# Gain rows of ten norms issued a stage sooner, the third weight chunk after a norm held in written order, and the odd mixer's bounds computed in the memory attention

## The chip, the cores and the metric

The kernel runs on one core of a Trainium2 chip. The metric is the device time of one execution in microseconds. One program computes a whole network for one sequence of 256 tokens; all weights come from device memory.

## What is computed

A residual `x` of 256 x 1024 floats passes two layers of a first block, a norm, two layers of a second block and a last norm. Each sublayer begins with an RMS norm whose gain is a row of 1024 floats.

```python
def rmsnorm(x, g):
    y = x * rsqrt(mean(x * x, axis=-1) + EPS)
    return y * g

# first block, twice: three attention branches, FFN, gated per-layer embedding
h = rmsnorm(x, mix_norm)
z = h @ w_in                       # attention branches a, b, c from z
x = x + (g_a * (o_a @ w_a) + g_b * (o_b @ w_b) + g_c * (o_c @ w_c)) @ w_out
h2 = rmsnorm(x, ffn_norm)          # FFN width 2816 = 22 x 128
x = x + (silu(h2 @ w_gate) * (h2 @ w_up)) @ w_down
x = x + sigmoid(rmsnorm(x, ple_norm) @ w_ple_gate) * (p_i @ w_ple_proj)
# then x = rmsnorm(x, final_norm)

# second block, layer 0 with the even mixer, layer 1 with the odd mixer
x = x + mixer(rmsnorm(x, norm_mix))
x = x + cross_attention(rmsnorm(x, norm_xattn), rmsnorm(mem, norm_mem))
x = x + peer_ffn(rmsnorm(x, norm_ffn))   # 16384 experts, 16 of them per head
# the odd mixer scales its gates with lb = softmax(hgrn_lb_logits, axis 0)[0]
```

## The kernel before

**Matmuls.** Everything is float32. A product is made of three TensorE passes: each operand is split into a rounded part `hi` and a remainder `lo`, and `mm3` issues hi x hi (L305), lo x hi (L306) and hi x lo (L307) into one PSUM bank. A line number as L305 is that of the kernel before.

**Weights.** `chunk` fetches 128 x 1024 floats of a weight (512 KB) by SyncE's queue into one of three `raw` buffers, casts it to `hi` on ScalarE (L289) and subtracts on VectorE to get `lo` (L290, on POOL for some), each again in three buffers. 24 matmuls of 256 columns, or 12 of 512, consume a chunk.

**Two forms of projection.** `lin_a` sums one 512-wide output block over all chunks of its contraction (eight for 1024 inputs) before its consumer runs. `lin_b` gets an output block of 128 features (transposed) out of each chunk, and after each block its `consume` copies from PSUM. The FFN is written like lin_b: for each column f a gate chunk (`ffg`) and an up chunk (`ffu`), 48 matmuls into `fps`, then Silu on ScalarE (L909), the product on VectorE (L910) and the split of the result into `hh` and `hl`; the down chunk of column f comes behind the matmuls of column f+1. In layer 0, `mem_norm` computes the RMS norm of the memory for the second block beside the FFN (Square L378, scaling L380).

**Norms.** Squares of the residual are summed on ScalarE (L420) as blocks of it are finished; v = sum + eps on VectorE (L429), r = v to the power -1/2 on POOL (L431), the scaling `xn = h * r * g` in four instructions on VectorE (L434), then 16 TensorE transposes (L389) into `trp`, and casts and subtractions from PSUM into the pair `xT` (`fTh`, `xTh`, `hTh` by the stage). `norm_t` does all that, and lets `fill` put independent matmuls (the memory's key and value projections) in front of the transposes. The gain row, broadcast to 128 partitions (512 KB), is loaded by `gain` when the norm is written: for most norms into a tile of a pool opened for this norm, whose memory was in use by the stage before; for the two mixers' norms into a `raw` buffer.

**What sets the order.** Code is written stage after stage, and a list scheduler then orders each engine's instructions by a model of their times, so that a weight's cast usually lands far ahead of where it was written. `keep_in_program_order(i)` takes one instruction out of that: it stays behind the instruction written just before it on its own engine. The engines issue strictly in the order so fixed. Memory tiles come from pools on a left and a right side; the residual `h` lies on the right.

**The odd mixer's bounds.** At the start of the odd mixer, L1473 to L1481 make `lb` and 1 - `lb` from two columns of 8 numbers per partition: subtract the maximum, two exponentials on ScalarE (L1476, L1477, with a table load), add, reciprocal, multiply.

Of the kernel before, what the change touches and what calls it, by code (L numbers as in the profile page):

```python
# [10 lines left out]
F32 = mybir.dt.float32  # L11
# [4 lines left out]
AF = mybir.ActivationFunctionType  # L16
OP = mybir.AluOpType
# [3 lines left out]
S, D, P = 256, 1024, 128  # L21
# [173 lines left out]
GAINS = {}  # L195


class Net:
    def __init__(self, ctx, tc, a, out):
        self.tc, self.nc, self.a, self.out = tc, tc.nc, a, out  # L200
        nc = self.nc
# [9 lines left out]
        self.memd = dp.tile([2, P, 8 * S], F32, name="memd")  # L211
        self.kvd = dp.tile([2, P, 4, D], F32, name="kvd")
        self.todo = []
        self.ks = None
        self.open_h()
        ctx.callback(lambda: self.hs.close())
# [12 lines left out]
        lo, hi = COLS["sconv0"][0], sum(COLS["mconvb"])  # L229
# [9 lines left out]
        with self.tc.tile_pool(name="mk", bufs=1) as mk:  # L239
            o, w = CONST["CM"][0], 3 * P  # L240
# [23 lines left out]
    def open_h(self):  # L264
        self.hs = ExitStack()
        hp = self.hs.enter_context(self.tc.tile_pool(name="hp", bufs=1, side="right"))
        self.h = hp.tile([P, 2, D], F32, name="h")

    def bank(self, name):

# [15 lines left out]

    def split(self, src, hi, lo, eng=None):

        self.nc.scalar.copy(out=hi, in_=src)  # L289
        (eng or self.nc.vector).tensor_tensor(out=lo, in0=src, in1=hi.bitcast(F32), op=OP.subtract)  # L290

    def chunk(self, ap, n, raw_only=False, eng=None):

        raw = self.wp.tile([P, 1024], F32, tag="raw", name="raw", bufs=3)
        self.nc.sync.dma_start(out=raw[:, :n], in_=ap)
        if raw_only:
            return raw[:, :n]
        hi = self.wp.tile([P, 1024], F32R, tag="hi", name="hi")
        lo = self.wp.tile([P, 1024], F32R, tag="lo", name="lo")
        self.split(raw[:, :n], hi[:, :n], lo[:, :n], eng)  # L300
        return hi[:, :n], lo[:, :n]

    def mm3(self, ps, lh, ll, rh, rl, start, stop):
# [53 lines left out]
    def rstd(self, ss, n, dim):  # L357
# [5 lines left out]
        nc.gpsimd.tensor_tensor(out=r, in0=v, in1=self.mhalf[:, :n], op=OP.pow)  # L363
        return r

    def gain(self, name, pool=None):
        if name == "mix_norm_0":
            return self.first
        g = self.wp.tile([P, D], F32, tag="raw", name="raw", bufs=3) if pool is None else pool.tile([P, D], F32, tag="gain", name="g", bufs=1)
        j = GAINS[name]  # L370
        self.nc.sync.dma_start(out=g, in_=self.a["gains"][j:j + 1, :].to_broadcast([P, D]))
        return g
# [25 lines left out]
    def norm_t(self, pool, gname, name, fill=0):  # L398
        dst = self.pair(pool, name, 8)
        with self.tc.tile_pool(name="nt", bufs=1) as tp:  # L400
            g = self.gain(gname, None if gname in ('norm_mix_2_0', 'norm_mix_2_1') else tp)
            xs = []
            for t in range(2):
                xs.append(tp.tile([P, D], F32, tag="xn", name="xn", bufs=2))
                self.rms_h(t, g, xs[t])
            fill() if callable(fill) else self.fill(fill)
            for k in range(0, 8, 4):
                for t in range(2):
                    self.trans(xs[t][:, k * P:(k + 4) * P], 4, t, [d[:, k:k + 4] for d in dst])
        return dst  # L410

    def add_h(self, b, t, ps, x=None):
# [178 lines left out]
    def first_layer(self, l):  # L591
        nc, a = self.nc, self.a
        with ExitStack() as st:
# [40 lines left out]
            mT = self.pair(pool("mt"), "mT", 8)  # L634
            for t in range(2):
                self.trans(merged[:, t], 8, t, mT)
            self.lin_a(mT, a[f"wout_{l}"], self.add_h)
        if l:
            self.kv_open(0, "v")
# [294 lines left out]
    def ple(self, l, xp, pr, fill):  # L934
        nc, a = self.nc, self.a
        xT = self.norm_t(xp, f"ple_norm_{l}", "pxT", fill)

        def cg(b, t, ps):
            sl = slice(b * 512, b * 512 + 512)
            g = xp.tile([P, 512], F32, tag="tmp", name="pg", bufs=2)  # L940
            nc.scalar.activation(out=g, in_=ps, func=AF.Sigmoid)
            nc.vector.tensor_tensor(out=g, in0=g, in1=pr[:, t, sl], op=OP.mult)
            self.add_h(b, t, g)
        self.lin_a(xT, a[f"pleg_{l}"], cg)


# [60 lines left out]
    def kv_close(self):  # L1007
        self.fill(1 << 20)
        if self.ks is not None:
            self.ks.close()  # L1010
            self.ks = None

    def mem_attn(self, l):
        nc, a = self.nc, self.a
        with ExitStack() as st:
# [54 lines left out]
            for t in range(2):  # L1070
                turn(0, t, Ps[t])
            Ps = [scores(1, t) for t in range(2)]
            outs(0)
            outs(1)
            for t in range(2):
                turn(1, t, Ps[t])
            outs(2)
            outs(3)
            self.lin_a(oT, a[f"xwo_{l}"], self.add_h)

    def softplus(self, pool, x, w):
# [32 lines left out]
    def even_mixer(self, xp, hT):  # L1114
# [48 lines left out]
        def project():  # L1163
            for kt in range(16):
# [4 lines left out]
                                 hi[:, n * 512:n * 512 + 512], lo[:, n * 512:n * 512 + 512], kt == 0, kt == 15)  # L1169
                yield 1  # L1170
        out = project()
        with st:
            self.ssd(sp_, c, hT, dt, cs, lg, yT, xb, xbc)
        with ExitStack() as st:
# [290 lines left out]
    def odd_mixer(self, xp, hT):  # L1465
        nc, a = self.nc, self.a
        with ExitStack() as st:
            pl = st.enter_context(self.tc.tile_pool(name="hg", bufs=1))
            c = self.tables(pl, "m01", "rst")

            T8 = lambda n: pl.tile([P, 8], F32, name="lb_" + n)
            mx, e0, e1, lb, ob = T8("m"), T8("0"), T8("1"), T8("b"), T8("o")
            nc.vector.tensor_tensor(out=mx, in0=self.col["lb0"], in1=self.col["lb1"], op=OP.max)  # L1473
            nc.vector.tensor_tensor(out=e0, in0=self.col["lb0"], in1=mx, op=OP.subtract)
            nc.vector.tensor_tensor(out=e1, in0=self.col["lb1"], in1=mx, op=OP.subtract)
            nc.scalar.activation(out=e0, in_=e0, func=AF.Exp)  # L1476
            nc.scalar.activation(out=e1, in_=e1, func=AF.Exp)  # L1477
            nc.vector.tensor_tensor(out=e1, in0=e0, in1=e1, op=OP.add)
            nc.vector.reciprocal(e1, e1)
            nc.vector.tensor_tensor(out=lb, in0=e0, in1=e1, op=OP.mult)  # L1480
            nc.vector.tensor_scalar(ob, lb, -1.0, 1.0, op0=OP.mult, op1=OP.add)  # L1481
            big = lambda n: pl.tile([P, 8, S], F32, name=n)
            f, k, q = big("hf"), big("hk"), big("hq")

# [128 lines left out]
            self.lin_a(oT, a["od_out"], self.add_h)  # L1613


# [227 lines left out]
```

## Time and profile before

| | us |
|---|---|
| three runs | 3420.84, 3422.93, 3423.55 (median 3422.93) |
| profiled execution, its own time | 3420.93 |
| its span | 3419.2 |
| TensorE busy | 3283.9 (96%) |
| VectorE busy | 2251.0 (66%) |
| ScalarE busy | 1759.0 (51%) |
| DMA, mean over the span | 167 GB/s |

TensorE is the busy engine; 570 MB of weights stream beside it. A busy share is a mean over all stages. PE is TensorE's matmul, DVE VectorE, ACT ScalarE, SP SyncE, which issues the DMAs. "Granted clock" is the share of TensorE's full clock (2.4 GHz; half of it is 1.2 GHz) that it got in a stretch. In rows of instructions, the bracket at a row's end is how long that engine stood idle before it, and what ended the idle time.

### The profile page before, as it was taken

Reading aid. Unit: us, or ns where it says so; the run is one execution under the profiler, and the core shown is the slowest. Engines: PE = TensorE matmul, PEld = TensorE weight load, DVE = VectorE, ACT = ScalarE, POOL = GpSimd, SP = SyncE. Lnnn points to the kernel's source line nnn. Section 1 sums busy time; section 2 is a strip of 40 time slices with the busy share of each in tenths; the row PEclk is TensorE's granted clock in tenths of the full one; section 3 lists DMA queues with packets and bytes.
Section 4 is the critical chain, followed back from the end, with each engine's and each line's share of the span. In section 5 each row is a group of like instructions: output and inputs, shape, how many; then the busy total and the mean of one; then the engine's idle time right before and its main releaser. Section 6 shows DMA issues by size and latency. Waiting matters only on the chain.

```text
span 3419.2 us, 53950 instructions
## 1 busy us (share of the span) xinstructions
PE 3283.9 (96%) x20870; PEld 2901.5 (85%) x20870; DVE 2251.0 (66%) x3881; ACT 1759.0 (51%) x3222; POOL 240.1 (7%) x159
## 2 busy tenths in 40 slices
PE   8999999989999999989999999999999899999999
PEld 6768998767997988888988999988888898899998
DVE  6666556756556776589965555567658996555555
ACT  4545445544445554445954444456444495444444
POOL 0000000000000000065000000000005500000000
PEclk9999999989999999999999999999999999999999
DMA  5345666445555345543255555555544315555555
GB/s 188 114 141 188 221 205 193 133 130 169 174 188 180 132 156 175 174 141 124 72 192 186 188 188 186 189 192 174 183 156 148 124 58 192 189 186 189 186 187 177
DMA packets 161105, 570.00 MB, mean 167 GB/s; under 512 B 18256, under 2 KB 23760, under 8 KB 159824
## 3 DMA queue, kind: packets, MB, share of 16 engines
q1 hardware_dynamic: 160848, 566.56, 50.1%
q8 instruction: 163, 2.67, 0.3%
q14 instruction: 94, 0.77, 0.1%
HBM read 557.05 MB, written 9.44 MB: 166 GB/s over the span
## 4 chain that ended last, share of the span: by engine, by line
PE 62%; DVE 11%; ACT 2%; DMA 1%; issue 1%; POOL 0%; DVEq 0%; POOLq 0%; ACTq 0%; SPq 0%
PE pacc L305 7%; PE pacc L307 7%; PE pacc L306 7%; PE aps L305 5%; PE aps L306 4%; PE aps L307 4%; PE ps L307 3%; PE ps L305 3%; PE ps L306 3%; PE gps L1697 3%; PE ps L1690 2%; PE fps L305 1%; PE fps L306 1%; PE fps L307 1%; DVE G L1783 1%
## 5 line engine op out<-in xcount | busy, mean ns | idle before, releaser
L290 DVE TENSOR_TENSOR lo<-raw,hi 128x1024 fp32r<-128x1024 f32 (+3 forms) x906 | 1102.3, 1218 | 769.7 <-ACT hi L289 764.9
L289 ACT CAST hi<-raw 128x1024 fp32r<-128x1024 f32 (+1 forms) x978 | 1019.1, 1044 | 919.5 <-issue 213.8
L305 PE MATMUL pacc<-hi,pwh 128*128 128x512 f32 x1024 | 404.4, 395 | 0.1
L307 PE MATMUL pacc<-hi,pwl 128*128 128x512 f32 x1024 | 403.7, 394 | 0.0
L306 PE MATMUL pacc<-lo,pwh 128*128 128x512 f32 x1024 | 402.9, 393 | 0.0
L305 PE MATMUL aps<-xTh,hi 128*128 128x256 f32 x1296 | 365.2, 282 | 0.9 <-ACT G L1700 0.9
L306 PE MATMUL aps<-xTl,hi 128*128 128x256 f32 x1296 | 365.0, 282 | 0.0
L307 PE MATMUL aps<-xTh,lo 128*128 128x256 f32 x1296 | 363.7, 281 | 0.0
L305 PE MATMUL ps<-xTh,hi 128*128 128x256 f32 x960 | 277.0, 289 | 16.4 <-ACT hi L289 12.5
L307 PE MATMUL ps<-xTh,lo 128*128 128x256 f32 x960 | 276.4, 288 | 15.2 <-POOL lo L290 15.2
L289 ACT CAST pwh<-G 128x256 fp32r<-128x256 f32 x256 | 103.9, 406 | 342.6 <-DVE G L1705 213.8
L306 PE MATMUL ps<-xTl,hi 128*128 128x256 f32 x960 | 275.5, 287 | 1.2 <-DVE xTl L290 1.2
L305 PEld LDWEIGHTS aps<-xTh,hi 128*128 128x128 f32 x1296 | 243.8, 188 | 7.8 <-ACT G L1700 1.3
L306 PEld LDWEIGHTS aps<-xTl,hi 128*128 128x128 f32 x1296 | 243.7, 188 | 7.2
L307 PEld LDWEIGHTS aps<-xTh,lo 128*128 128x128 f32 x1296 | 243.8, 188 | 0.0
L307 PEld LDWEIGHTS pacc<-hi,pwl 128*128 128x128 f32 x1024 | 192.4, 188 | 45.7 <-DVE pwl L290 0.3
L305 PEld LDWEIGHTS pacc<-hi,pwh 128*128 128x128 f32 x1024 | 192.6, 188 | 39.1 <-ACT pwh L289 1.0
L306 PEld LDWEIGHTS pacc<-lo,pwh 128*128 128x128 f32 x1024 | 193.1, 189 | 37.9
L290 POOL TENSOR_TENSOR lo<-raw,hi 128x1024 fp32r<-128x1024 f32 x72 | 192.4, 2681 | 179.1 <-ACT hi L289 178.6
L305 PE MATMUL fps<-fTh,hi 128*128 128x256 f32 x704 | 199.6, 284 | 4.8 <-ACT fTh L289 4.8
L305 PEld LDWEIGHTS ps<-xTh,hi 128*128 128x128 f32 x960 | 186.2, 194 | 18.1 <-ACT hi L289 13.3
L307 PEld LDWEIGHTS ps<-xTh,lo 128*128 128x128 f32 x960 | 186.3, 194 | 16.5 <-POOL lo L290 16.3
(653 smaller groups left out, 6958.0 us busy)
## 6 DMA issues: line engine op xcount, KB each, us to landing
raw<-in_pu_dram SPq DMA_DIRECT2D x256, 512.0 KB, 3.3
raw<-in_pv_dram SPq DMA_DIRECT2D x256, 512.0 KB, 3.3
raw<-in_wbg_dram SPq DMA_DIRECT2D x48, 512.0 KB, 3.6
raw<-in_ffg_dram SPq DMA_DIRECT2D x44, 512.0 KB, 3.6
raw<-in_ffu_dram SPq DMA_DIRECT2D x44, 512.0 KB, 3.4
raw<-in_ffd_dram SPq DMA_DIRECT2D x44, 512.0 KB, 3.8
raw<-in_win_dram SPq DMA_DIRECT2D x36, 512.0 KB, 3.3
raw<-in_pwq_dram SPq DMA_DIRECT2D x32, 512.0 KB, 3.3
```

The costliest lines, as they stand in the source:

```text
L289: self.nc.scalar.copy(out=hi, in_=src)
L290: (eng or self.nc.vector).tensor_tensor(out=lo, in0=src, in1=hi.bitcast(F32), op=OP.subtract)
L305: mm(ps, lhsT=lh, rhs=rh, start=start, stop=False)
L306: mm(ps, lhsT=lh, rhs=rl, start=False, stop=False)
L307: mm(ps, lhsT=ll, rhs=rh, start=False, stop=stop)
L1690: nc.tensor.matmul(pi, lhsT=w[:, k * P:k * P + P], rhs=xT32[:, k], start=k == 0, stop=k == 7)
L1697: nc.tensor.matmul(ps[:, t * P:t * P + P], lhsT=A[:, t], rhs=B[:, t], start=True, stop=True)
L1783: nc.vector.tensor_tensor(out=cv[:, h], in0=vv[:, h, 0, :, None].to_broadcast([P, 16, 16]), in1=vv[:, h, 1, None, :].to_broadcast([P, 16, ...
```

## The change

1. `gain_ahead(name)` loads a norm's gain row into one buffer that lies in the pool of the residual, and `gain` later takes it from there. It is called for ten of the fifteen rows that `gain` loads: the ffn and ple norms of both layers, the second layer's first norm (`mix_norm_1`), `final_norm`, and the query and PEER norms of the second block. The call stands before the last projection of the stage ahead of the norm (for the ple norm, behind the FFN's norm; for the query norm of layer 0, ahead of the even mixer's recurrences).
2. `norm_t` sets a counter to zero at its end; `chunk` counts, and keeps cast and subtraction of the third chunk in written order on their engines.
3. The odd mixer's bounds move into `lower_bounds`, called in the memory attention of the second block's first layer, between the scores of its second head and the outputs of its first; the two exponentials are held in written order there. 

```diff
@@ chunk
-        self.split(raw[:, :n], hi[:, :n], lo[:, :n], eng)
+        ins = self.split(raw[:, :n], hi[:, :n], lo[:, :n], eng)
+        self.since += 1
+        if self.since == 3:
+            for i in ins:
+                self.tc.keep_in_program_order(i)
@@
+    def gain_ahead(self, name):
+        g = self.hp.tile([P, D], F32, tag="gain", name="g", bufs=1)
+        j = GAINS[name]
+        self.nc.sync.dma_start(out=g, in_=self.a["gains"][j:j + 1, :].to_broadcast([P, D]))
+        self.ahead[name] = g
@@ gain
+        if name in self.ahead:
+            return self.ahead.pop(name)
@@ norm_t, at its end
+        self.since = 0
@@ calls, each ahead of the projection beside it
+            self.gain_ahead(f"ffn_norm_{l}")
             self.lin_a(mT, a[f"wout_{l}"], self.add_h)
...
             xT = self.norm_t(xp, f"ffn_norm_{l}", "fT", fill)
+            self.gain_ahead(f"ple_norm_{l}")
...
+        self.gain_ahead("final_norm" if l else "mix_norm_1")
         self.lin_a(xT, a[f"pleg_{l}"], cg)
...
+            self.gain_ahead(f"norm_ffn_2_{l}")
             self.lin_a(oT, a[f"xwo_{l}"], self.add_h)
...
         out = project()
+        self.gain_ahead("norm_xattn_2_0")
...
+            self.gain_ahead("norm_xattn_2_1")
             self.lin_a(oT, a["od_out"], self.add_h)
@@ mem_attn
             Ps = [scores(1, t) for t in range(2)]
+            if l == 0:
+                self.lower_bounds()
             outs(0)
@@ odd mixer
-            mx, e0, e1, lb, ob = T8("m"), T8("0"), T8("1"), T8("b"), T8("o")
-            nc.vector.tensor_tensor(out=mx, in0=self.col["lb0"], in1=self.col["lb1"], op=OP.max)
...
-            nc.scalar.activation(out=e0, in_=e0, func=AF.Exp)
-            nc.scalar.activation(out=e1, in_=e1, func=AF.Exp)
...
+            lb, ob = self.lbs
```

The number of instructions stays the same on all engines but ScalarE, which has one table load less. The order changes around the norms. In the rows below `hi<-raw` is a weight's cast, `lo<-raw,hi` its subtraction; the code's later lines stand a few further down in the changed kernel (L289 is L292 there, L909 is L930, L290 is L293, L1030 is L1068).

ScalarE at the FFN of layer 0, from the casts of the normed input on, before:

```order
L289 CAST fTh<-trp 128x4x128 x4
L289 CAST hi<-raw 128x1024 x2
L378 ACTIVATE xn,ss<-mem 128x1024
L289 CAST hi<-raw 128x1024
L909 ACT_TABLE_LOAD
L909 ACTIVATE sg<-fps 128x256
L378 ACTIVATE xn,ss<-mem 128x1024
L289 CAST hh<-sg 128x256
L289 CAST hi<-raw 128x1024 x2
```

and in the changed kernel:

```order
L292 CAST fTh<-trp 128x4x128 x4
L396 ACTIVATE xn,ss<-mem 128x1024
L930 ACT_TABLE_LOAD
L930 ACTIVATE sg<-fps 128x256
L396 ACTIVATE xn,ss<-mem 128x1024
L292 CAST hh<-sg 128x256
L292 CAST hi<-raw 128x1024 x5
```

The casts of column 1's gate and up chunk (and of column 0's down chunk) stood ahead of Silu of column 0; now they stand behind `hh` of column 0.

ScalarE at the query projection of the second block's layer 0 (`xTh` is the normed input, `mqT` the copy of one 128-feature block of queries), before:

```order
L289 CAST xTh<-trp 128x4x128 x4
L289 CAST hi<-raw 128x1024
L1030 ACTIVATE mqT<-ps 128x256
L289 CAST hi<-raw 128x1024 x2
L1030 ACTIVATE mqT<-ps 128x256
L289 CAST hi<-raw 128x1024
L1030 ACTIVATE mqT<-ps 128x256
```

and in the changed kernel:

```order
L292 CAST xTh<-trp 128x4x128 x4
L1068 ACTIVATE mqT<-ps 128x256 x2
L292 CAST hi<-raw 128x1024 x3
L1068 ACTIVATE mqT<-ps 128x256
L292 CAST hi<-raw 128x1024 x2
L1068 ACTIVATE mqT<-ps 128x256
```

The third chunk's cast stood ahead of the first block's copy; now it stands behind the second block's.

VectorE in the even mixer, around `lg`, the last step of the softplus chain (`sp_q` are its steps, `cacc` and `xb` those of a convolution), before:

```order
L290 TENSOR_TENSOR lo<-raw,hi 128x1024
L1095 SCALAR_TENSOR_TENSOR sp_q<-sp_q,sp_z_10615 128x40
L1112 SCALAR_TENSOR_TENSOR xb<-xpad,cacc 128x256
L1096 SCALAR_TENSOR_TENSOR sp_q<-sp_q,sp_z 128x40
L1108 TENSOR_SCALAR cacc<-xpad,cl 128x256
L1097 SCALAR_TENSOR_TENSOR sp_q<-sp_q,sp_m 128x40
L1110 SCALAR_TENSOR_TENSOR cacc<-xpad,cl,cacc 128x256
L1151 TENSOR_TENSOR lg<-sp_q,na 128x2x16
L1152 TENSOR_SCALAR lg<-sp_q 128x2x4
```

and in the changed kernel:

```order
L1136 SCALAR_TENSOR_TENSOR sp_q<-sp_q,sp_z_10615 128x40 x3
L1153 SCALAR_TENSOR_TENSOR xb<-xpad,cacc 128x256
L1137 SCALAR_TENSOR_TENSOR sp_q<-sp_q,sp_z 128x40
L1138 SCALAR_TENSOR_TENSOR sp_q<-sp_q,sp_m 128x40
L1192 TENSOR_TENSOR lg<-sp_q,na 128x2x16
L1193 TENSOR_SCALAR lg<-sp_q 128x2x4
L293 TENSOR_TENSOR lo<-raw,hi 128x1024 x3
```

The subtractions of chunks 3 to 5 were spread among the chain's steps; now all three stand behind `lg`.

## Rows read from the trace of the kernel before

**Rows 1.** Page: the span, and the engines' busy time, share and instructions.
```profile
span 3419.2 us, 53950 instructions
PE 3283.9 (96%) x20870; PEld 2901.5 (85%) x20870; DVE 2251.0 (66%) x3881; ACT 1759.0 (51%) x3222; POOL 240.1 (7%) x159
```
**Rows 2.** Page, costliest groups: count, busy us, mean ns; idle time before and releaser.
```profile
L290 DVE TENSOR_TENSOR lo<-raw,hi 128x1024 fp32r<-128x1024 f32 (+3 forms) x906 | 1102.3, 1218 | 769.7 <-ACT hi L289 764.9
L289 ACT CAST hi<-raw 128x1024 fp32r<-128x1024 f32 (+1 forms) x978 | 1019.1, 1044 | 919.5 <-issue 213.8
```
**Rows 3.** Windows: length; busy us of PE, PEld, DVE, ACT, POOL; granted clock; DMA.
```profile
309.50:321.40 11.90, 11.75 (x96) 11.49 (x96) 5.96 (x9) 7.54 (x12) 0.55 (x1) 1.00 0.87 304
848.60:854.90 6.30, 1.90 (x18) 1.68 (x17) 2.23 (x4) 3.60 (x7) 0.00 (x0) 0.83 0.67 222
854.90:860.40 5.50, 5.49 (x27) 5.25 (x28) 1.66 (x3) 0.22 (x1) 0.00 (x0) 0.57 0.29 95
...
1085.00:1094.00 9.00, 4.82 (x32) 4.28 (x31) 7.38 (x15) 6.88 (x17) 1.23 (x4) 0.87 0.50 154
...
1412.00:1430.00 18.00, 15.36 (x123) 14.52 (x122) 14.27 (x18) 8.82 (x16) 1.07 (x2) 1.00 0.84 289
...
2530.00:2541.00 11.00, 3.67 (x17) 3.07 (x17) 6.90 (x12) 3.82 (x9) 1.06 (x2) 0.69 0.76 244
```
**Rows 4.** Timeline of ACT, FFN of layer 0: start and length in us.
```profile
309.84 1.09 ACT L289 CAST hi<-raw 128x1024 fp32r<-128x1024 f32 x1
...
316.31 1.06 ACT L378 ACTIVATE xn<-mem 128x1024 f32<-128x1024 f32 x1 [2.34 <-DMA mem<-in_mem_dram]
...
318.42 1.28 ACT L909 ACT_TABLE_LOAD   x1
319.71 0.39 ACT L909 ACTIVATE sg<-fps 128x256 f32<-128x256 f32 x1
...
321.04 0.39 ACT L289 CAST hh<-sg 128x256 fp32r<-128x256 f32 x1
```
**Rows 5.** Timeline of DVE, same stretch.
```profile
320.13 0.42 DVE L910 TENSOR_TENSOR sg<-sg,fps 128x256 f32<-128x256 f32 x1 [0.47 <-ACT sg L909]
...
321.81 1.28 DVE L380 SCALAR_TENSOR_TENSOR xn<-mem,r,g 128x1024 f32<-128x1024 f32 x1
```
**Rows 6.** Timeline of POOL, same stretch.
```profile
321.47 0.83 POOL L363 TENSOR_TENSOR r<-v,mhalf 128x1 f32<-128x1 f32 x1 [3.12 <-DVE v L361]
```
**Rows 7.** Groups of ACT by form: count, busy us, mean ns.
```profile
L1030 ACT ACTIVATE mqT<-ps 128x256 f32<-128x256 f32 x16 | 6.0, 377 | 0.0
...
L1486 ACT ACTIVATE hf<-ps 128x256 f32<-128x256 f32 x8 | 3.1, 384 | 0.7 <-PE ps L307 0.7
```
**Rows 8.** Timeline of DVE, final norm and even mixer's start.
```profile
1084.56 2.74 DVE L434 SCALAR_TENSOR_TENSOR h<-h,r,g 128x512 f32<-128x512 f32 x4 [3.83 <-DMA g<-in_gains_dram]
...
1108.96 1.22 DVE L290 TENSOR_TENSOR lo<-raw,hi 128x1024 fp32r<-128x1024 f32 x1
...
1115.69 0.18 DVE L1151 TENSOR_TENSOR lg<-sp_q,na 128x32 f32<-128x32 f32 x1
```
**Rows 9.** Timeline of ACT, FFN of layer 1.
```profile
851.87 1.04 ACT L289 CAST hi<-raw 128x1024 fp32r<-128x1024 f32 x1 [2.66 <-DMA raw<-in_ffg_dram]
```
**Rows 10.** Timeline of DVE, PEER norm of layer 1.
```profile
2534.81 2.74 DVE L434 SCALAR_TENSOR_TENSOR xn<-h,r,g 128x512 f32<-128x512 f32 x4 [3.02 <-DMA g<-in_gains_dram]
```
**Rows 11.** Timeline of POOL, same norm.
```profile
2531.81 1.06 POOL L431 TENSOR_TENSOR r<-v,mhalf 128x1 f32<-128x1 f32 x2 [75.05 <-DVE v L429]
```
**Rows 12.** Timeline of PE, query projection of layer 1.
```profile
2466.89 0.62 PE L305 MATMUL ps<-xTh,hi 128*128 128x256 f32 x3 [0.68 <-ACT xTh L289]
2468.37 0.39 PE L306 MATMUL ps<-xTl,hi 128*128 128x256 f32 x1 [0.86 <-DVE xTl L290]
```
**Rows 13.** Timeline of ACT, odd mixer's start.
```profile
2303.17 1.04 ACT L289 CAST hi<-raw 128x1024 fp32r<-128x1024 f32 x1 [1.35 <-DMA raw<-in_od_f_dram]
```
**Rows 14.** Waits of PE: us in total, times, longest.
```profile
PE psb L307 <- DVE lo L290: 4.3, 4, 1.7
```

More of the change, by code (lines that the diff above doesn't have):

```diff
@@ L213, in __init__ @@
         self.todo = []
+        self.since = 0
+        self.ahead = {}
         self.ks = None
@@ L267, in open_h @@
         self.h = hp.tile([P, 2, D], F32, name="h")
+        self.hp = hp
     def bank(self, name):
@@ L287, in split @@
     def split(self, src, hi, lo, eng=None):
-        self.nc.scalar.copy(out=hi, in_=src)
-        (eng or self.nc.vector).tensor_tensor(out=lo, in0=src, in1=hi.bitcast(F32), op=OP.subtract)
+        h = self.nc.scalar.copy(out=hi, in_=src)
+        l = (eng or self.nc.vector).tensor_tensor(out=lo, in0=src, in1=hi.bitcast(F32), op=OP.subtract)
+        return h, l
     def chunk(self, ap, n, raw_only=False, eng=None):
@@ L409, in norm_t @@
                     self.trans(xs[t][:, k * P:(k + 4) * P], 4, t, [d[:, k:k + 4] for d in dst])
+        self.since = 0
         return dst
@@ L1011, in kv_close, with lower_bounds @@
             self.ks = None
+    def lower_bounds(self):
+        nc = self.nc
+        T8 = lambda n: self.cp.tile([P, 8], F32, name="lb_" + n)
+        mx, e0, e1, lb, ob = T8("m"), T8("0"), T8("1"), T8("b"), T8("o")
+        nc.vector.tensor_tensor(out=mx, in0=self.col["lb0"], in1=self.col["lb1"], op=OP.max)
+        nc.vector.tensor_tensor(out=e0, in0=self.col["lb0"], in1=mx, op=OP.subtract)
+        nc.vector.tensor_tensor(out=e1, in0=self.col["lb1"], in1=mx, op=OP.subtract)
+        for e in (e0, e1):
+            self.tc.keep_in_program_order(nc.scalar.activation(out=e, in_=e, func=AF.Exp))
+        nc.vector.tensor_tensor(out=e1, in0=e0, in1=e1, op=OP.add)
+        nc.vector.reciprocal(e1, e1)
+        nc.vector.tensor_tensor(out=lb, in0=e0, in1=e1, op=OP.mult)
+        nc.vector.tensor_scalar(ob, lb, -1.0, 1.0, op0=OP.mult, op1=OP.add)
+        self.lbs = lb, ob
     def mem_attn(self, l):
@@ L1469, in odd_mixer @@
             c = self.tables(pl, "m01", "rst")
-            T8 = lambda n: pl.tile([P, 8], F32, name="lb_" + n)
-            mx, e0, e1, lb, ob = T8("m"), T8("0"), T8("1"), T8("b"), T8("o")
-            nc.vector.tensor_tensor(out=mx, in0=self.col["lb0"], in1=self.col["lb1"], op=OP.max)
-            nc.vector.tensor_tensor(out=e0, in0=self.col["lb0"], in1=mx, op=OP.subtract)
-            nc.vector.tensor_tensor(out=e1, in0=self.col["lb1"], in1=mx, op=OP.subtract)
-            nc.scalar.activation(out=e0, in_=e0, func=AF.Exp)
-            nc.scalar.activation(out=e1, in_=e1, func=AF.Exp)
[L1478 to L1481, printed above, removed]
+            lb, ob = self.lbs
             big = lambda n: pl.tile([P, 8, S], F32, name=n)
```

## Prediction

> **What bounds the kernel now.** I read the page's busy times first. TensorE is busy for 96% of a span of 3419.2 us [rows 1], so the change can move the time only where TensorE stands still or where its clock falls. Next I asked for the cost of feeding it. Each weight chunk needs one cast on ScalarE (1.04 us) and one subtraction on VectorE (1.22 us), 978 and 906 times [rows 2], before its third matmul can run. Matmul work per 128x1024 chunk is 2.86 us: the 96 matmuls of two FFN columns ran in 11.90 us with only a short wait at their start, 0.119 us each [rows 3]. So both feeders are faster than TensorE as long as they may run ahead, and a feeder that must not run ahead costs TensorE a full chain of cast and subtraction. Then I went through the places that the diff touches, norm by norm, and asked there which wait ends last. The profiled execution took 3420.93 us; the median of the runs is 3422.93, 2 us more, inside their spread of 2.7.
>
> **The pin on the third chunk.** The pin puts cast and subtraction of the third chunk after a norm behind whatever was written just before on the same engine. In the projections that sum over eight chunks (ple gate, input projection) that is the second chunk, and nothing waits; I price those at 0. In the others the consumer of the first two chunks is written before the third one, so the third chunk can now only be cast when TensorE has finished all it has. That holds at eight places.
>
> *FFN of layer 0.* In the trace the cast of chunk 3 runs at 309.84, long before Silu at 319.71 [rows 4], and TensorE never stops between f=0 and f=1. Afterwards the ScalarE order is Square of mem, table load, Silu, Square, hh, then this cast. The first Square began at 316.31 when its DMA landed [rows 4], which is after the 48 matmuls of f=0 end (about 315.6, half of the 96 [rows 3]). So: Square to 317.4, table load 1.28 to 318.7, Silu 0.39 to 319.1, a second Square (1.06) to 320.1, hh 0.39 to 320.5, cast 1.05 to 321.4 (starts overlap by 0.1). VectorE has in front of its subtraction the product with Silu (0.42), two scalings of mem (1.28 each), hl, and a power on POOL that the second scaling needs (0.83) [rows 5, 6]: product to 319.5, scaling to 320.8, hl to 321.2, power to 322.2, scaling to 323.4, subtraction to 324.6. The third matmul of f=1 could have run at 315.9: **+8.8**. If mem landed early and only Silu, product, hh, hl, power, scaling and subtraction stood in a row the price would be 5.4; with mem's DMA a load later, 10.3.
>
> By that row the table load holds ScalarE for 1.28 and Silu starts 0.01 later. The Trainium skill (ScalarE: Activation LUTs, What ACT_TABLE_LOAD costs) adds a drain of 1.38 us to every switch. By it this term would be 10.2 and the sum 1.4 larger; the trace shows no such drain here, and I go by the trace.
>
> *FFN of layer 1.* No mem work there: Silu 0.39, product 0.42, hh 0.39, cast 1.05, subtraction 1.22, less two matmuls that need only the cast (0.24), and 0.3 for hand-overs: **+3.5**.
>
> *The two query projections and the two PEER projections.* One copy of a 128x256 PSUM block (0.38 [rows 7]), cast 1.05, subtraction 1.22, less 0.24: 2.4, with the hand-over 2.5, four times: **+10.0**. Bounds 2.2 and 2.9 each.
>
> *Odd mixer.* hf and hk (0.38 each [rows 7], overlapping to 0.66) ahead of cast and subtraction: **+2.8**.
>
> *Even mixer.* ScalarE isn't held, VectorE is: the subtraction of chunk 3 now stands behind lg, the end of the softplus chain. In the trace that subtraction ran at 1108.96 and lg at 1115.69 [rows 8]. This eats what the norm gives there; it is priced with the norm below.
>
> **The gain rows loaded ahead.** The 512 KB rows are the same, ten of fifteen are issued one stage sooner. It matters where the scaling waited for its row, or where the third chunk's cast stood ahead of the transposes' casts.
> - FFN of layer 1: TensorE works 1.90 of the 6.30 us from 848.60 [rows 3], because a weight cast that waited 2.66 for its DMA stands on ScalarE ahead of fTh [rows 9]. The pin takes that cast away: fTh can follow the transposes, **-4.0**. The half clock behind this wait (27 matmuls in 5.50 us where 0.119 each would be 3.2 [rows 3]) goes too: **-2.3**.
> - Even mixer: final_norm's scaling waited 3.83 for its row until 1084.56 [rows 8]. Early by about that, the transposes and the first xbc chunk move forward by 5. But chunk 2 is then late by its DMA, and chunk 3 waits for lg, which I work out to 1107.3 (about 12 softplus steps after chunk 2's first matmuls, interleaved with the convolution): chunk 3's matmuls start at about 1108.5, and by chunk 5 the lead is gone: **0**, bounds -5 and +4.
> - PEER of layer 1: the scaling waited 3.02 for its row until 2534.81, r was there at 2532.9 [rows 10, 11]. Gain at least 1.9, at most 3.9 (without the cast and the subtraction that ran ahead of the squares and of v): **-3.5**, nearer to the upper end since both are pinned away.
> - PEER of layer 0 and queries of layer 1, the same cast out of the way: **-0.9**, and **-1.6** (the waits of 0.68 and 0.86 [rows 12]).
> - The other norms didn't wait for their rows: 0. The issue costs SP 0.3 to 0.4 us each as before; a row that goes out ahead of a weight chunk can delay it, which I keep for the range (+0 to +2).
>
> **The odd mixer's bounds.** Seven tiny VectorE steps, two exponentials and a table load of 1.28 leave the odd mixer's start. ScalarE waited for a weight DMA there until 2303.17 [rows 13], so nothing becomes earlier: 0. In the memory attention they stand beside other exponentials: 0.
>
> **The clock.** New stalls can cost more than their length. TensorE fell to the half clock behind the 4.4 us of idle time before 854.90 (a granted 0.57 in the 5.5 us after it); the 9 us from 1085 with 4.2 idle show 0.87; the 18 us from 1412, with 2.6 idle in several pieces, stay at 1.00 [rows 3]. I take 2.3 behind the long stall of FFN 0, as measured there, 1.7 behind the shorter one of FFN 1, and 1.0 for the four of 2.5 together, which lie between the two cases: **+5**.
>
> **Sum.** Losses 8.8 + 3.5 + 10.0 + 2.8 = 25.1; gains 4.0 + 2.3 + 3.5 + 0.9 + 1.6 = 12.3; clock 5. 3420.9 + 25.1 - 12.3 + 5 = 3438.7. Against a median that lies 2 us above the profiled execution it would be 3440.7; the measured runs reach down to 3420.84, so I give **3438**.
>
> **Rivals.**
> 1. *No change.* The even mixer keeps its lead of 5, no new stall lowers the clock, FFN 0 costs its lower bound: 3438.7 - 5 - 5 - 3.4 = 3425. For it: the stretch with 2.6 idle at 1.00. Against it: the subtraction behind lg.
> 2. *Faster.* The place is the front of four norms. All that TensorE loses there goes: in FFN 1 6.3, in the even mixer about 10 (4.2 of the 9 us from 1085, the four waits of psb on its subtractions, 4.3 together [rows 14], and the clock), in PEER 1 7.3 of the 11 us from 2530 [rows 3], 2.5 in PEER 0, 1.5 in the queries: 28. The pins' stalls are at their lower bounds, 5.4 + 3.2 + 4 x 2.2 + 2.5 = 20. That gives 3413. It decides from gains of about 27 on; against it stands that a norm has squares, v, r, scaling, transposes and casts in a row even with its row at hand, so PEER 1 can't lose its whole 7.3.
> 3. *The clock falls behind each new stall.* Besides the two FFN stalls the other six cost 1.7 each instead of 1.0 together: 3438.7 + 9 = 3448. The rows with 0.87 and with 1.00 lie on both sides of such a stall.
>
> The Trainium skill (TensorE: Matmul & The Clock Gate, What's actually happening) says that the gate goes by how busy the array was of late; by that alone rival 3 would hold wherever a stall is long enough, and the traced stretch at 1.00 shows that short ones are free.
>
> **How the numbers follow.** Chances: the forecast 0.53, rival 3 0.15, no change 0.20, faster 0.12. The range: from the lower bounds (no clock loss, FFN 0 at 5.4, even mixer -5, PEER gain 3.9) 3424, lowered to 3420 to take in the no-change case; from the upper ones (FFN 0 at 10.3, even mixer +4, PEER gain 1.9, clock +9 more) 3455, cut to 3452 since they won't all come together. About what a measurement of this kernel can tell from no change is 0.2%, 6.8 us: faster 0.12, within 0.20, slower 0.68.
>
> **What would show it.** Right: in the changed kernel's trace a TensorE wait of 8 to 9 us on a subtraction in FFN 0 right after f=0, with the weight cast after hh; waits of about 2.5 on lo in both query and both PEER projections; the wait before FFN 1's first matmul gone and one of 3.5 three us later; final_norm's scaling starting at once on its row, and a wait on lo behind lg. Wrong: the third chunk's casts before the consumers, or TensorE waits there under 1 us; then the gains stand alone and the kernel is faster.

## The result, and the profile after

The changed kernel took 3440.43 us in the median of four runs (3438.8 to 3446.18), the kernel before 3421.89 (3420.62 to 3423.55): 1.0057 of before, 95% interval 1.0042 to 1.0071. It is 18.5 us slower; 3438 was forecast. The profiled execution has a span of 3437.0 us against 3419.2 [rows 1].

Page of the changed kernel, the span and the engines' busy time:

```profile
span 3437.0 us, 53932 instructions
PE 3295.3 (96%) x20870; PEld 2909.9 (85%) x20870; DVE 2253.1 (66%) x3881; ACT 1758.0 (51%) x3221; POOL 239.6 (7%) x159
```

The engines do the same work as in [rows 1]; TensorE's busy time is 11.4 us longer with the same 20870 matmuls, at a mean granted clock of 0.980 instead of 0.984: more of them ran at the half clock. Thus 11.4 of the 17.8 us between the two spans are matmuls that took longer, and 6.4 are time in which TensorE stood idle. Where the time went is found by comparing the start of the same matmul in two traces (the n-th of 20870) at the borders of the stages. Each number is how much longer, in us, a stage took than in the trace of the kernel before; the column "idle" is the part of it in which TensorE stood still (the stage's length less PE's busy time in it), and the rest is matmuls that took longer:

| stage (us of before) | changed | of it idle | forecast | before, profiled again |
|---|---|---|---|---|
| FFN of layer 0 (308 to 330) | +9.4 | +7.0 | +8.8, clock +2.3 | -0.3 |
| FFN of layer 1 (845 to 880) | 0.0 | -1.3 | -6.3 +3.5, clock +1.7 | -0.7 |
| final norm and even mixer's start (1074 to 1125) | +3.8 | +0.6 | 0 | -0.2 |
| queries of layer 0 (1345 to 1385) | +0.8 | +0.7 | +2.5 | +0.1 |
| PEER norm and projection 0 (1412 to 1450) | +2.5 | +0.9 | -0.9 +2.5 | +0.2 |
| odd mixer's start (2301 to 2345) | +5.7 | +2.1 | +2.8 | +1.5 |
| queries of layer 1 (2440 to 2500) | -0.6 | -0.8 | -1.6 +2.5 | -0.1 |
| PEER norm and projection 1 (2525 to 2565) | -0.4 | -1.3 | -3.5 +2.5 | +0.5 |

These add to +21.2, of which 8.0 are idle time and 13.2 longer matmuls. The other stages gave back 3.4, which makes up the 17.8 between the two spans; in the second trace of the unchanged kernel they gave back 3.3 too, so that lies in the trace of before and not in the change. The last column says how to take such numbers: it is the unchanged kernel against itself (experiment e10). Stages without an edit differ there by 1.2 (start), -2.4 (compressed keys of layer 1) and -2.5 (routing of layer 1), and the odd mixer by 1.5.

**FFN of layer 0.** Timeline of ScalarE in the changed kernel (start, length, idle time before it and what ended it), to be held against [rows 4]:

```profile
317.20 1.06 ACT L396 ACTIVATE xn<-mem 128x1024 f32<-128x1024 f32 x1 [6.39 <-DMA mem<-in_mem_dram]
...
318.36 1.28 ACT L930 ACT_TABLE_LOAD   x1
319.66 0.38 ACT L930 ACTIVATE sg<-fps 128x256 f32<-128x256 f32 x1
...
320.98 0.39 ACT L292 CAST hh<-sg 128x256 fp32r<-128x256 f32 x1
321.27 1.99 ACT L292 CAST hi<-raw 128x1024 fp32r<-128x1024 f32 x2
```

VectorE there, and TensorE:

```profile
322.82 1.28 DVE L398 SCALAR_TENSOR_TENSOR xn<-mem,r,g 128x1024 f32<-128x1024 f32 x1 [0.73 <-POOL r L372]
324.02 2.35 DVE L293 TENSOR_TENSOR lo<-raw,hi 128x1024 fp32r<-128x1024 f32 x2
```

```profile
316.42 0.28 PE L316 MATMUL fps<-fTh,lo 128*128 128x256 f32 x1
322.37 0.58 PE L314 MATMUL fps<-fTh,hi 128*128 128x256 f32 x1 [5.67 <-ACT hi L292]
...
324.26 0.79 PE L314 MATMUL facc<-hi,hh 128*128 128x512 f32 x1 [1.10 <-ACT hi L292]
325.29 0.58 PE L316 MATMUL fps<-fTh,lo 128*128 128x256 f32 x1 [0.24 <-DVE lo L293]
```

The raw chunk lay ready, but ScalarE stood 6.39 us for mem's DMA, and only behind Square, table load, Silu, the second Square and hh came the cast at 321.27, which had been at 309.84 [rows 4]. The subtraction waited for mem's second scaling. The third matmul of column 1 came at 325.29; without a wait it would have been due three matmuls after 316.42, at 316.78: 8.5 us, where 8.8 were worked out.

**FFN of layer 1.** ScalarE in the changed kernel:

```profile
857.17 2.06 ACT L292 CAST fTh<-trp 128x512 fp32r<-128x512 f32 x4
859.24 1.28 ACT L930 ACT_TABLE_LOAD   x1
865.01 0.38 ACT L930 ACTIVATE sg<-fps 128x256 f32<-128x256 f32 x1 [4.49 <-PE fps L316]
...
866.19 2.94 ACT L292 CAST hi<-raw 128x1024 fp32r<-128x1024 f32 x3
```

TensorE there:

```profile
867.28 0.58 PE L314 MATMUL fps<-fTh,hi 128*128 128x256 f32 x1 [2.31 <-ACT hi L292]
...
868.54 0.58 PE L316 MATMUL fps<-fTh,lo 128*128 128x256 f32 x1 [0.47 <-DVE lo L293]
```

The wait in front of fTh [rows 9] is gone, and the casts of column 1 come behind Silu and hh instead. Both are worth 6 us, so nothing is left of the gain.

**Clock.** Windows of the changed kernel (length; busy us of PE, PEld, DVE, ACT, POOL; granted clock; DMA):

```profile
316.55:325.20 8.65, 1.74 (x5) 0.79 (x3) 4.55 (x8) 6.98 (x10) 1.10 (x2) 0.76 0.15 62
325.20:332.00 6.80, 6.71 (x46) 6.71 (x47) 3.54 (x4) 1.05 (x1) 0.00 (x0) 0.80 0.69 231
...
864.40:872.00 7.60, 4.82 (x23) 4.33 (x23) 4.34 (x5) 3.63 (x5) 0.00 (x0) 0.69 0.31 87
...
2327.00:2332.50 5.50, 5.50 (x34) 5.49 (x34) 3.01 (x5) 1.81 (x4) 0.00 (x0) 0.69 0.71 234
```

Behind each of the three longer stalls (both FFNs, odd mixer) TensorE ran part of the following work at the half clock: 46 matmuls took 6.71 us in the second window where 0.119 each would be 5.5, and 34 took 5.50 in the last one where they would be 4.0.

### The profile page after: what moved, and what is told of

Its sections match the earlier page's. It is cut to its first block, busy times and chain, and to the rows that moved or that the text cites. A ratio compares the mean times of both kernels' runs of the same rounds, so it can differ in the third digit from the quotient of the medians.

```text
span 3437.0 us, 53932 instructions
## 1 busy us (share of the span) xinstructions
PE 3295.3 (96%) x20870; PEld 2909.9 (85%) x20870; DVE 2253.1 (66%) x3881; ACT 1758.0 (51%) x3221; POOL 239.6 (7%) x159
## 4 chain that ended last, share of the span: by engine, by line
PE 61%; DVE 11%; ACT 2%; DMA 1%; issue 1%; POOL 0%; DVEq 0%; POOLq 0%; ACTq 0%; SPq 0%
PE pacc L314 7%; PE pacc L316 7%; PE pacc L315 7%; PE aps L314 5%; PE aps L315 4%; PE aps L316 4%; PE ps L314 3%; PE ps L316 3%; PE ps L315 3%; PE gps L1729 3%; PE ps L1722 2%; PE fps L316 1%; PE fps L315 1%; PE fps L314 1%; DVE G L1815 1%; ACT hi L292 1%
## 5 line engine op out<-in xcount | busy, mean ns | idle before, releaser
L293 DVE TENSOR_TENSOR lo<-raw,hi 128x1024 fp32r<-128x1024 f32 (+3 forms) x906 | 1101.5, 1218 | 769.0 <-ACT hi L292 763.8
L292 ACT CAST hi<-raw 128x1024 fp32r<-128x1024 f32 (+1 forms) x978 | 1018.2, 1044 | 883.9 <-issue 210.5
L292 ACT CAST pwh<-G 128x256 fp32r<-128x256 f32 x256 | 103.8, 406 | 342.2 <-DVE G L1737 213.9
L293 POOL TENSOR_TENSOR lo<-raw,hi 128x1024 fp32r<-128x1024 f32 x72 | 191.6, 2672 | 181.6 <-ACT hi L292 131.6
L316 PE MATMUL fps<-fTh,lo 128*128 128x256 f32 x704 | 200.0, 284 | 0.7 <-DVE lo L293 0.7
```

The source lines that it names most:

```text
L292: h = self.nc.scalar.copy(out=hi, in_=src)
L293: l = (eng or self.nc.vector).tensor_tensor(out=lo, in0=src, in1=hi.bitcast(F32), op=OP.subtract)
L316: mm(ps, lhsT=ll, rhs=rh, start=False, stop=stop)
```

## Experiments

All ratios are against the kernel before on the same chip, with 95% intervals. Stage numbers are differences to the trace of before, as in the table above.

**e1: the gain rows alone.** The changed kernel without its pin, and with the odd mixer's bounds where they were.

```diff
-        self.since += 1
-        if self.since == 3:
-            for i in ins:
-                self.tc.keep_in_program_order(i)
```

> The kernel before with the gain rows of the ten norms loaded ahead, no pin, bounds where they were. Theory A (the pins make the loss, the rows give a gain): the waits for gain rows in front of final_norm and of both PEER norms go, and the order ahead of the second FFN and of the second queries is cleared as well: 6 to 12 us faster than before, 3410 to 3416. Theory B (the rows issued ahead get in the way of weight loads, the pins cost nothing): 10 us or more slower than before.

Measured: 0.9988 (0.9979 to 0.9997). Theory A has the sign, but the gain is 3.4 us of 3422.85 and not 6 to 12. By stages: FFN 1 -6.3 as worked out, the even mixer's start +4.9 where a gain was expected, PEER 0 +1.6, PEER 1 -0.3. ScalarE at FFN 1 in this run:

```profile
849.30 2.05 ACT L292 CAST fTh<-trp 128x512 fp32r<-128x512 f32 x4
853.05 1.05 ACT L292 CAST hi<-raw 128x1024 fp32r<-128x1024 f32 x1 [1.69 <-DMA raw<-in_ffg_dram]
```

So the cast of [rows 9] that stood ahead of fTh moves behind it without any pin. With the gain row loaded ahead the scheduler orders the two the other way by itself.

The even mixer is the surprise. Its scaling and lg (VectorE), its first chunks and `cps`, the first matmul that needs lg (TensorE), and windows of the whole stage and of two stretches in it:

```profile
1073.81 2.74 DVE L449 SCALAR_TENSOR_TENSOR h<-h,r,g 128x512 f32<-128x512 f32 x4 [0.61 <-POOL r L446]
...
1112.94 0.18 DVE L1170 TENSOR_TENSOR lg<-sp_q,na 128x32 f32<-128x32 f32 x1
```

```profile
1092.98 0.39 PE L310 MATMUL psb<-hTh,hi 128*128 128x256 f32 x1 [1.67 <-ACT hi L292]
1095.46 0.58 PE L310 MATMUL psb<-hTh,hi 128*128 128x256 f32 x1 [1.75 <-ACT hi L292]
1113.25 1.04 PE L1175 MATMUL cps<-lg,cst 128*128 128x20 f32 x4 [3.86 <-DVE lg L1171]
```

```profile
1068.11:1123.99 55.88, 46.25 (x335) 43.94 (x334) 42.38 (x91) 28.76 (x56) 2.81 (x11) 0.88 0.52 164
1094.40:1101.10 6.70, 5.64 (x26) 5.64 (x27) 3.49 (x9) 2.59 (x5) 0.10 (x1) 0.50 0.74 229
1113.20:1118.00 4.80, 4.75 (x22) 4.75 (x23) 2.79 (x10) 0.42 (x1) 0.00 (x0) 0.50 0.30 106
```

The same stage in the kernel before:

```profile
1074.02:1125.01 50.99, 42.97 (x335) 40.51 (x333) 40.97 (x90) 28.97 (x56) 3.72 (x11) 0.97 0.53 171
```

The scaling no longer waits for its row (0.61 for r instead of 3.83 for the DMA [rows 8]). Yet TensorE is idle for 9.6 us of the stage instead of 8.0, and busy with the same 335 matmuls for 46.2 instead of 43.0. Behind the two waits for casts it gets through the chunks that are written ahead of cps without the later waits of [rows 14], and then stands 3.86 us in one piece for lg. VectorE makes lg even later, 44.8 us after the stage's start, where it was 41.7 before [rows 8]. The half clock follows in two places, behind the two waits of 1.67 and 1.75 (0.50 from 1094.40 to 1101.10) and behind the long one (0.50 from 1113.20 on).

**e2: the pin alone.** The kernel before with the counter and the pin, rows and bounds as before.

> The kernel before with the pin of the third chunk alone. Theory A: stalls of TensorE at the first FFN (about 9), the second FFN, the odd mixer (3 to 6) and both PEER projections (2.5 each), less what the casts give that no longer stand ahead of the norm's own casts: 15 to 25 us slower than before, 3437 to 3447. Theory B: within 3 us of before.

Measured: 1.0068 (1.0054 to 1.0081), 23.1 us: theory A. Stages: FFN 0 +9.7, FFN 1 -0.1, even mixer's start +4.3, PEER 0 +2.1, odd mixer +5.0, PEER 1 +2.5, queries +0.9 and -0.6. At FFN 1 the pin alone also takes away the wait of [rows 9]; the casts of column 1 come behind hh:

```profile
859.78 2.05 ACT L292 CAST fTh<-trp 128x512 fp32r<-128x512 f32 x4
...
868.79 2.94 ACT L292 CAST hi<-raw 128x1024 fp32r<-128x1024 f32 x3
```

The even mixer loses 4.3 us to the pin alone, 4.9 to the row alone and 3.8 to both, so the losses don't add. In all three TensorE waits for lg (2.33 here, 3.86 in e1, 2.27 in the changed kernel), and the stage's granted clock is 0.88 to 0.91 instead of 0.97.

**e3: the odd mixer's bounds alone.**

> The kernel before with the odd mixer's bounds made in the memory attention, nothing else. Theory A: ScalarE waits for a weight load at the odd mixer's start anyway, so within 2 us of before. Rival: the table load that goes was on the path to the second weight cast there, 1.3 to 2.5 us faster.

Measured: 1.0003 (0.9993 to 1.0012), the odd mixer's start -0.1. The table load taken off ScalarE buys nothing, since the next weight comes by DMA at its own time [rows 13].

**e4: the pair held behind the norm's own casts.** The pinned pair follows the last cast and subtraction of the norm's transposes, not what was written just before it.

```diff
-            for i in ins:
-                self.tc.keep_in_program_order(i)
+            for i, p in zip(ins, self.norm_last):
+                if i.ins.engine == p.ins.engine:
+                    self.tc.add_manual_dep(i.ins, p.ins.name, ...)   # issue order only
```

> The changed kernel with one thing different: cast and subtraction of the third chunk are held behind the last cast and subtraction of the norm's own transposes, and no longer behind the consumers of the first two chunks. Theory A: all stalls of the pins go and all gains stay: 8 to 15 us faster than before, 3407 to 3414. Theory B: as slow as the changed kernel, 3437 to 3443.

Measured: 0.9981 (0.9972 to 0.9990), 6.2 us faster than before, less than the 8 to 15 expected. In its trace the even mixer keeps its loss (+4.2) and a new one turns up in the attention of layer 1 (+4.9, e9). They are the likely reason, but not a shown one: the traced execution, 3410.01, is the fastest of eleven and lies where it was expected with both losses in it. All pins' stalls are gone: FFN 0 -0.1, FFN 1 -6.0, odd mixer -0.1, queries -0.1 and -1.4.

**e5: the changed kernel without the pin in the two FFNs.**

> The changed kernel with the pin left out in the two FFNs only. If the FFN pins cost what the stages of the traces say (9.4 in layer 0, 6.2 in layer 1 against the run with gain rows alone), this is 15 to 16 us faster than the changed kernel: 3424 to 3426. By the prediction's own terms (8.8 + 2.3 and 3.5 + 1.7) it would be 16.3. If instead the time lost is made up elsewhere (the later FFN columns), less than 8.

Measured: 1.0012 (1.0003 to 1.0021), that is 0.0045 of 3424 or 15 us below the changed kernel, as the stages say (FFN 0 -0.1, FFN 1 -5.9). The FFN pins are four fifths of the whole loss.

**e6: mem's Squares held back.** The changed kernel with the Squares of the memory's norm kept in written order.

```diff
+        if late:
+            self.tc.keep_in_program_order(i)   # i: the Square of a memory half
```

> The changed kernel with the Squares of the memory's norm held in written order, so that they come six and twelve FFN columns later and no longer stand between the first FFN's transposes and Silu. Theory A1 (the long stall of the first FFN is the wait for mem's load plus Square, table load and scalings ahead of the pinned pair): the stall falls from 8.9 to about 3.5, the first FFN's stage from 9.4 to 6 over before, and the kernel is 3 to 4 us faster than the changed kernel, 3436 to 3437. Rival (pin alone makes it, mem's steps fit beside): no change from 3440.

ScalarE and TensorE at FFN 0:

```profile
318.57 0.41 ACT L292 CAST hh<-sg 128x256 fp32r<-128x256 f32 x1 [0.49 <-DVE sg L933]
318.88 1.99 ACT L292 CAST hi<-raw 128x1024 fp32r<-128x1024 f32 x2
```

```profile
319.98 0.39 PE L314 MATMUL fps<-fTh,hi 128*128 128x256 f32 x1 [2.32 <-ACT hi L292]
...
321.24 0.39 PE L316 MATMUL fps<-fTh,lo 128*128 128x256 f32 x1 [0.76 <-DVE lo L293]
```

Measured: the stall falls to 2.32 + 0.76 and the stage from +9.4 to +5.0, so theory A1 holds for the stall: about half of it was mem's work ahead of the pinned pair (TensorE's idle time in the stage falls from 7.5 to 3.6). The kernel doesn't gain the 3 to 4 us that were expected: 1.0050 (1.0035 to 1.0065), which its interval doesn't tell from the changed kernel's 1.0057. From 330 to 470 us the FFN takes 3.5 us longer than in the kernel before, 0.1 less in the changed one; mem's steps stand there now, and TensorE waits twice for mem's scaling, 1.7 us in all.

**e7: e4 without final_norm's row loaded ahead.**

```diff
-        self.gain_ahead("final_norm" if l else "mix_norm_1")
+        if not l:
+            self.gain_ahead("mix_norm_1")
```

> The version with the pair held behind the norm's own casts, without the gain row of final_norm loaded ahead. Theory C (an earlier final norm makes the even mixer slower: TensorE gets through its first five chunks sooner, then waits 3.9 us in one piece for lg and falls to half clock): the stage from final_norm to 1125 us loses its +4.2, and the kernel is about 4 us faster than with that row, 3412 to 3413. Rival D (the row loaded ahead for the queries, inside the even mixer, does it, or chance): no change, 3416 to 3417.

Measured: 0.9961 (0.9947 to 0.9975). The stage from final_norm on goes from +4.2 to -0.1, and TensorE's idle time in it from 9.2 to 6.8: theory C as to the wait. The argument rests on the stage; the intervals of the whole kernel (this one and e4's) touch. TensorE there waits in pieces of 1.6 and 1.9, and no wait for lg shows:

```profile
1083.69 0.63 PE L409 MATMUL trp<-cst,xn 128*128 128x128 f32 x4 [1.59 <-DVE xn L456]
...
1105.37 0.38 PE L318 MATMUL psb<-hTh,lo 128*128 128x256 f32 x1 [1.90 <-DVE lo L293]
```

**e8: e4 with six xbc chunks written ahead of cps.**

```diff
-        self.take(xbc, 3)
+        self.take(xbc, 4)
         cps = self.bank("cps")
```

> The version with the pair held behind the norm's own casts, with all gain rows ahead, and one more xbc chunk written ahead of the matmuls that need lg (six chunks instead of five). Theory C: 2.9 us of work cover the 3.9 us wait for lg, the clock stays up, and the kernel is 5 to 7 us faster than without, 3409 to 3412. Rival D: the wait only moves, within 2 us of 3416.

Measured: 0.9956 (0.9942 to 0.9970), 15 us faster than before. The stage is at -1.4 with final_norm's row ahead, with 6.8 us idle and a granted clock of 0.97: one chunk's matmuls cover the wait for lg, as theory C has it. e7 and e8 can't be told apart by their times.

**e9: e8 without the hold at mix_norm.**

```diff
-        self.since = 0
+        self.since = 3 if gname.startswith("mix_norm") else 0
```

In e4, e7 and e8 the stretch from 560 to 700 us takes 3.7 to 5.8 longer. The trace of e8 shows why, a wait on the held subtraction, ahead of which a copy on VectorE waits for a DMA:

```profile
560.63 0.39 PE L317 MATMUL ps<-lo,hTh 128*128 128x256 f32 x1 [2.51 <-DVE lo L293]
```

```profile
559.08 0.23 DVE L888 COPY cw2d<-cw 128x128 f32<-128x128 f32 x1 [4.30 <-DMA cw<-in_cw2k_dram]
559.23 0.22 DVE L889 COPY cw2d<-cw 128x128 f32<-128x128 f32 x1
559.36 1.22 DVE L293 TENSOR_TENSOR lo<-raw,hi 128x1024 fp32r<-128x1024 f32 x1
```

> The version with six xbc chunks, with the pair behind the norm's casts everywhere but at mix_norm, where the trace of that version shows a wait of 2.4 us on the third chunk's subtraction at 557 us and 3.4 us of half clock behind it. Theory E: that hold alone costs the 4 to 6 us of the stage, so about 4 us faster than with it, 0.9944 of before, 3404 to 3407. Rival: the stage's time comes from the earlier gain row, no change.

Measured: the stretch is at +0.1 and the wait is gone, so theory E holds for the stage. The half clock that the expectation names is that of e4's trace; in e8's the granted clock stays at 1.00 behind the wait. The time, 0.9960 (0.9945 to 0.9975), is not better than e8's. Other stages of this one trace are 1.2 to 2.6 later than in e8's, about as much as two traces of one kernel differ; whether the hold costs the kernel 4 us isn't settled.

**e10: the kernel before once more.**

> The kernel before, unchanged, for a second profile: how far single stages differ between two executions of the same program. If stages that no edit touches (the two compressed-key stages, the rest of the even mixer, routing) differ here by 1 to 2.5 us too, such steps between two kernels mean nothing; the FFNs, the odd mixer and the even mixer's start should agree within 0.5.

Measured: 1.0004 (0.9992 to 1.0015); the stages are in the last column of the table. The FFN of layer 0 differs by 0.3, the even mixer by 0.2. The FFN of layer 1 (0.7) and the odd mixer (1.5 longer) don't agree within 0.5, so about 4 of the odd mixer's 5.7 in the changed kernel are the pin's. Two traces are too few to bound the scatter: in e3, whose edit touches neither place, the even mixer's start is 1.5 and the PEER stage of layer 1 2.4 longer than before, with TensorE idle only 0.4 and 0.1 longer. So in the table's stages TensorE's idle time repeats better than the length; in the routing of layer 1 it doesn't, the -2.5 there is idle time.

## Why the prediction was right, and which of its terms were not

**The pin as the main cost: right.** e2 and e4 show the cause from both sides: the pin alone costs 23 us, and moving it behind the norm's own casts takes all of it away; e5 puts four fifths of the loss into the two FFNs. That the time came within 3 us of 3438 is luck: the terms for idle time were too large and those for the clock too small, by about the same amount (see Clock).

**FFN of layer 0: right in size and by its steps.** Square at 317.2 when mem landed, table load, Silu, hh, cast, and the subtraction behind mem's second scaling; e6 takes mem out and half of the stall goes. The stage was 9.4 against 8.8 + 2.3: 7.0 of idle time and 2.4 of longer matmuls. So the 2.3 for the clock has the right size, but only about 1.2 of it came behind the stall; the rest lies within the 8.5, where three matmuls ran between the waits. The table load holds ScalarE 1.28 us and Silu starts 0.02 later. The drain that the Trainium skill adds (ScalarE: Activation LUTs, What ACT_TABLE_LOAD costs) shows in this trace no more than in that of before.

**FFN of layer 1: the gain right, the pin's price too small.** The gain of 6.3 is there (e1: 4.1 of idle time and 2.2 of clock, where 4.0 and 2.3 were worked out). The pin does take the cast from ahead of fTh, as the forecast has it (e2), but the row loaded ahead does so too (e1). So on top of the row the pin only loses: 0.0 instead of -6.3, where 3.5 + 1.7 were forecast. It is 2.8 of idle time and 3.4 of clock: 23 matmuls take 4.82 us of the window from 864.40.

**Even mixer: the path right, the clock left out.** Forecast 0, because the early norm's lead of 5 would be eaten by the subtraction behind lg; measured +3.8. VectorE and the whole stage in the changed kernel:

```profile
1087.67 2.74 DVE L453 SCALAR_TENSOR_TENSOR h<-h,r,g 128x512 f32<-128x512 f32 x4 [0.61 <-POOL r L450]
...
1117.18 0.19 DVE L1192 TENSOR_TENSOR lg<-sp_q,na 128x32 f32<-128x32 f32 x1
...
1117.36 3.49 DVE L293 TENSOR_TENSOR lo<-raw,hi 128x1024 fp32r<-128x1024 f32 x3
```

```profile
1081.96:1136.71 54.75, 46.16 (x335) 43.46 (x334) 42.78 (x90) 28.90 (x56) 2.98 (x11) 0.91 0.54 173
```

The scaling starts as soon as r is there, lg is made 35.2 us after the stage's start (33.3 by the forecast's 1107.3, 41.7 before), and the three subtractions stand behind it. TensorE's idle time is 8.6 us instead of 8.0, so the lead is eaten as worked out. The step that failed is that the clock was put at nothing here: the same 335 matmuls are busy for 46.2 us instead of 43.0, at 0.91 instead of 0.97.

Without the hold on the subtraction (e1, e4) the lead is lost another way. I followed the chunks only, to where block 5 ends, and not to cps, the next matmul, which needs lg. There lg is made later than before, and TensorE waits 3.86 us for it. e7 (no row) and e8 (one more chunk of cover) each remove that wait from e4; neither was run with the changed kernel's pin, so they don't explain its 3.8.

**Queries: mis-sized.** Forecast +2.5 each for the pin, measured +0.8 in layer 0, and -0.6 in layer 1, where it is -1.3 to -1.4 without the pin's stall (e4, e7 to e9). I read ScalarE's order and not TensorE's. In layer 0 the scheduler put the scores of the first queries into the gap:

```profile
1367.73 1.89 PE L1078 MATMUL msc<-mkv,mqT 128*128 128x256 f32 x8
...
1370.25 0.39 PE L314 MATMUL ps<-xTh,hi 128*128 128x256 f32 x1 [0.39 <-ACT hi L292]
```

Eight score matmuls take 1.6 us of the wait, and 0.39 and a few tenths are left.

**Odd mixer: mis-sized, +5.7 for +2.8.** ScalarE in the changed kernel, and TensorE:

```profile
2324.49 0.38 ACT L1518 ACTIVATE hk<-ps 128x256 f32<-128x256 f32 x1
2324.76 2.94 ACT L292 CAST hi<-raw 128x1024 fp32r<-128x1024 f32 x3
```

```profile
2325.86 0.39 PE L314 MATMUL ps<-hTh,hi 128*128 128x256 f32 x1 [1.68 <-ACT hi L292]
...
2326.80 0.39 PE L314 MATMUL ps<-hTh,hi 128*128 128x256 f32 x1 [0.45 <-ACT hi L292]
```

The wait is 2.1 in all, where 2.8 was forecast. Behind it the clock fell (0.69 for 5.5 us), 1.5 more, and 1.5 is what the unchanged kernel itself differs by there. In e6 the stage has the same 2.1 more of idle time and is only 3.1 longer, so what the clock adds differs from execution to execution.

**PEER: both terms too large.** The sum of both stages was forecast as +0.6 and measured as +2.1. PEER 1: the scaling no longer waits for its row, as [rows 10] had it. Its stage scatters (-0.3 in e1 and e7, -1.0 in e9, -2.5 in e4 and e8), but TensorE's idle time in it is 2.4 to 2.9 shorter in all five: that is the gain, for which 3.5 was forecast. In the changed kernel it is 1.3 shorter, so the pin costs 1.2 there, not 2.5. PEER 0: the pin costs as much (idle +0.9, against -0.3 in e4), and the clock the rest of the +2.5. With the row ahead the wait for the split of the normed input, 1.72 before, is 2.91 (e1) or 2.33 (the others); why, is open.

**Bounds: right**, 0 (e3).

**Clock: the term that failed.** The forecast's 17.8 us above the profiled execution are 15.1 of idle time (25.1 less 10.0 of the gains) and 2.7 of clock (5 less the 2.3 of FFN 1). Measured in the eight stages are 8.0 of idle time and 13.2 of longer matmuls. Of the idle time above all the four pins of 2.5 were too large; they cost about 3.3 together (the changed kernel against e4). Of the clock, 1.0 was forecast outside the FFNs, and the six stages there lost 9.6 (1.4 of it, at the odd mixer, the unchanged kernel has in e10 too). That is nearly the sum of rival 3 (1.7 at each of six stalls), though not its rule: both queries stayed at 1.00, and the even and odd mixers lost over 3 each. It is no accident of one trace, though the size differs: the same eight stages have 10.9, 11.5 and 8.2 of longer matmuls in e2, e5 and e6, which hold the pin too, 6.1 in e1 (the rows alone) and -0.3 to 1.2 in e4 and e7 to e9.

**The signs.** In FFN 0 the time came as 5.67 and 1.10 on casts and 0.24 on the subtraction, and not as one wait. FFN 1's was 2.31 and 0.47, 6.4 us behind its first matmul and not three. Waits of 2.5 on lo are at neither the queries nor the PEER projections; under 1 us, a sign of being wrong, holds for the queries. final_norm's scaling started as was said; the wait behind it was for lg itself:

```profile
1117.51 1.04 PE L1197 MATMUL cps<-lg,cst 128*128 128x20 f32 x4 [2.27 <-DVE lg L1193]
```

## What to carry to other kernels

An instruction pinned to the order in which code is written stands behind whatever was written before it, consumers included; pin it behind the very instructions that it should follow (here the norm's own casts), and read the orders of all engines at each place, the waiting one's too. A step that comes earlier is worth something only as far as the slowest of the next join's inputs comes earlier; in e1 and e4 the row loaded ahead moved matmuls up to a join whose other input did not come earlier, until one more chunk of work was put ahead of the join (e8). Forecast idle time and clock separately and compare each with its own measurement: here their errors cancelled in the sum. Where the effect is 0.5% of the time, profile the unchanged kernel more than once before single stages are explained, and compare TensorE's idle time in a stage as well as its length.

## What the runs showed of the hardware

The same waits can cost a different amount of clock in two executions. The PEER stage of layer 1 in e4 and in e7, which have the same code there and the same 5.7 us of idle time:

```profile
2519.40:2556.87 37.47, 31.75 (x237) 30.05 (x236) 21.32 (x24) 16.12 (x26) 1.10 (x2) 0.95 0.58 196
```

```profile
2517.88:2557.62 39.74, 34.02 (x238) 32.31 (x236) 21.33 (x24) 16.13 (x26) 1.10 (x2) 0.87 0.57 186
```

The matmuls take 2.3 us longer at 0.87 than at 0.95; the 1.5 at the odd mixer in e10 and the 1.5 and 2.4 in e3 are of this kind too. Short waits aren't safe either: in e1 two of 1.67 and 1.75 us close together were followed by 6.7 us at 0.50, the half clock of 1.2 GHz, and one of 3.86 by 4.8 us at 0.50, while behind one of 2.51 in e8 the clock stayed at 1.00. So these runs don't show that one long wait costs more than the same time in pieces. The Trainium skill (TensorE: Matmul & The Clock Gate, HAM oscillation — how this bites in real kernels) describes how waits for data make the clock go down and up; these rows agree, and show that with TensorE busy for 96% of the span it still costs some microseconds per place. Not expected was how much executions of one program scatter on one core: the kernel before ran from 3417.0 to 3429.9 us in 27 runs, with stages that differ by 2.5 us between two traces.
